# Two output projections of an encoder layer: norm weight applied while PSUM is emptied, scaling and residual in one operation, low parts of weights on another engine

## The chip, the cores and the metric

The kernel runs on one core of a Trainium2 chip. The metric is the device time of one execution in microseconds (us); times are medians over runs. The engines of a core, as the profile names them, are PE (TensorE, the matrix unit), DVE (VectorE), ACT (ScalarE), POOL (GpSimd) and SP (SyncE, which issues the DMAs here). Each engine works through its own queue in order; semaphores tie the queues together.

## The reference

One layer of an encoder trunk, 1024 tokens of width D = 1024, all in float32. Each of its three sub-layers stands between a norm before it and a norm behind it, and is added to the residual stream:

```
def _rms_norm(x, gain):
    y = x * rsqrt(mean(x * x, axis=-1) + EPS)
    return y * gain

mix = concat([attn_o, dn_o]) @ w_out            # mixer: windowed attention and DeltaNet
x = x + _rms_norm(mix, g_mix_post)
c = cross_attention(_rms_norm(x, g_cross_pre), _rms_norm(mem, g_mem), w_cq, w_ckv, w_co)
x = x + _rms_norm(c, g_cross_post)              # c ends with  o @ w_co
f = swiglu(_rms_norm(x, g_ffn_pre), w_gate_up, w_down)
x = x + _rms_norm(f, g_ffn_post)
```

The change concerns the two lines with `g_mix_post` and `g_cross_post`: the projections by `w_out` and `w_co` (1024 x 1024 each), the norm behind them and the residual addition.

## The kernel before

**Float32 in three products.** TensorE multiplies in a reduced format here. Each operand is split into a high part (a cast on ScalarE, line 102) and a low part (what is missing, line 103 or 106), and each product is made of three: high x high, high x low, low x high. A weight is loaded by `load_w` (lines 118 to 126): a DMA of 512 KB into `wraw`, a cast to `whi` on ScalarE, a subtraction to `wlo` on the engine that the caller names, VectorE if none. All three tiles have two buffers, and this happens with a priority 300 instructions ahead of the place where it stands in the program.

**The projection.** `mid_gemm` (lines 959 to 1000) does one half of the tokens (512, four tiles `z` of 128 tokens) for one projection. It is called four times: `w_out` halves 0 and 1, then, after the cross attention, `w_co` halves 0 and 1. Each call goes over two chunks `ch` of 512 output columns, and for each of them over four pieces `kp` of the weight; so there are 8 weight loads in a call and 32 in all, with `wlo` made by GpSimd. A chunk fills four PSUM banks (`pmg`). Each is then read twice: ScalarE squares it and sums the squares into one column of `sss[t]` (line 979), and VectorE copies it to `z` (line 980).

**The post norm.** After both chunks, for each of the four tiles: the residual `xr` is fetched (line 986); GpSimd adds the two sums (line 988) and forms `prs`, the reciprocal root of the mean, in two tiny operations (`rstd_of`, lines 157 and 158: scale and add EPS, then raise to -0.5); VectorE multiplies `z` by `prs` and by the gain `gpost` in one operation (line 991) and adds `xr` in another (line 992); `z` is written out (line 993). Then the next sub-layer's norm is prepared in the same loop: ScalarE squares `z` (line 995), GpSimd forms `pr` through the same two lines, and ScalarE scales into `xr` (line 998). `gpost` comes from `gpost_tile` (lines 952 to 955), a DMA that repeats the gain over 128 partitions. The same function serves the FFN's norm at the end of the kernel, where line 1300 multiplies the gain by sqrt(D); that norm leaves out the division by D in its statistics and has D x EPS instead (line 1328).

**What stands around it.** The normed tiles are transposed on TensorE (`ptn`) and split into operands. Between the halves lie the products of the cross attention: the query projection `cross_q` (`pcq`, line 254, with `wlo` from GpSimd), the scores `pcs`, their maximum and softmax (`cmx`, `cpr`, lines 1060 to 1068), the transposes `pct` with their split (`cph`, `cpl`) and `pco`. Behind the second call with `w_co`, the normed tiles become the FFN's operands T1 to T4 in a chain on VectorE and ScalarE (lines 1124 to 1141), while the first gate and up products are begun early (lines 1149 to 1171: `pA`, its copy `m`, the activation at line 1170). Then the FFN's main loop takes differences of weights (`pair_weights`, lines 1187 to 1211) and runs to the end.

**Order.** The order of instructions on each engine isn't written out by hand: a scheduler with its own estimates of durations lays it down when the kernel is built, so that a changed cost or engine can reorder what stands near it. `wraw`, `whi` and `wlo` have two buffers each, `z` and `xr` four, `pmg`, `pcq` and `pA` share four PSUM banks in this stage.

Of the kernel before, what the change touches and what calls it, by code (L numbers as in the profile page):

```python
# [10 lines left out]
F32 = mybir.dt.float32  # L11
# [3 lines left out]
ALU = mybir.AluOpType  # L15
# [4 lines left out]
P = 128  # L20
S = 1024
D = 1024
# [4 lines left out]
EPS = 1e-6  # L27
# [48 lines left out]
def tile_hybrid_block(  # L76
# [6 lines left out]
    nc = tc.nc  # L83
# [15 lines left out]
    def split(hi, lo, src, scale=None, eng=None):  # L99

        if scale is None:
            nc.scalar.copy(hi, src)  # L102
            (eng or nc.vector).tensor_tensor(lo, src, f32(hi), ALU.subtract)  # L103
        else:
            nc.scalar.activation(hi, src, AF.Identity, scale=scale)
            nc.vector.scalar_tensor_tensor(lo, src, scale, f32(hi), ALU.mult, ALU.subtract)

    def pool(name, bufs, **kw):
        return tc.tile_pool(name=name, bufs=bufs, reuse_waits="tile", **kw)
# [8 lines left out]
    def load_w(src, k, n, eng=None):  # L118

        with tc.high_priority(AHEAD):  # L120
            raw = wp.tile([P, k, n], F32, tag="wraw", name="wraw")
            nc.sync.dma_start(raw, src.rearrange("(k p) n -> p k n", p=P))
            hi = wp.tile([P, k, n], F32R, tag="whi", name="whi")
            lo = wp.tile([P, k, n], F32R, tag="wlo", name="wlo")
            split(hi, lo, raw, eng=eng)
        return hi, lo
# [4 lines left out]
    mhalf = cst.tile([P, 16], F32, name="mhalf")  # L131
# [22 lines left out]
    def rstd_of(rs, ss, n, eps):  # L154

        w = ss.shape[-1]
        nc.gpsimd.tensor_scalar(rs, ss, n, eps, ALU.mult, ALU.add)
        nc.gpsimd.tensor_tensor(rs, rs, mhalf[:, :w], ALU.pow)  # L158
# [31 lines left out]
    pss = ExitStack()  # L190
# [13 lines left out]
    for hf in range(2):  # L204
        hi = hx.tile([P, KT, HALF], F32R, name=f"hhi{hf}")
        lo = hx.tile([P, KT, HALF], F32R, name=f"hlo{hf}")
        for j in range(4):
            t = 4 * hf + j
# [4 lines left out]
            ss = t1.tile([P, 1], F32, tag="ss", name="ss", bufs=4)  # L213
            nc.scalar.activation(junk, xt, AF.Square, accum_out=ss)
            rs = t1.tile([P, 1], F32, tag="rs", name="rs", bufs=4)
# [88 lines left out]
    for hf in range(2):  # L304
        pp = pg.tile([P, 512], F32, tag="pg", name="pg")
# [644 lines left out]
            split(his[:, k, :], los[:, k, :], pt, gain(gname, k))  # L950

    def gpost_tile(pool_, g):
        t = pool_.tile([P, D], F32, tag="gpost", name="gpost", bufs=1)
        nc.sync.dma_start(t, g[0].partition_broadcast(P))
        return t

    XR = 4

    def mid_gemm(tz, act, w, gp, res, dst, hf, between=None):


        zs = [tz.tile([P, D], F32, tag="z", name="z", bufs=4) for _ in range(4)]
        sss = [tz.tile([P, 2], F32, tag="zss", name="zss", bufs=8) for _ in range(4)]
        for ch in range(2):
            cs = slice(ch * 512, (ch + 1) * 512)
            if ch and between:
                between()
            pp = [pg.tile([P, 512], F32, tag="pg", name="pmg") for _ in range(4)]
            for kp in range(4):
                whi, wlo = load_w(w[kp * 256:(kp + 1) * 256, cs], 2, 512, nc.gpsimd)  # L970
                for t in range(4):
                    tt = slice(t * P, (t + 1) * P)
                    for kk in range(2):
                        k = 2 * kp + kk
                        for i, (w_, a) in enumerate(((whi, 0), (whi, 1), (wlo, 0))):
                            nc.tensor.matmul(pp[t], act[a][:, k, tt], w_[:, kk, :], start=(k == 0 and i == 0),  # L976
                                             stop=(k == KT - 1 and i == 2))
            for t in range(4):
                nc.scalar.activation(zs[t][:, cs], pp[t], AF.Square, accum_out=sss[t][:, ch:ch + 1])
                nc.vector.tensor_copy(zs[t][:, cs], pp[t])  # L980
        xn = []
        for t in range(4):
            tok = slice(hf * HALF + t * P, hf * HALF + (t + 1) * P)
            z = zs[t]
            xr = tz.tile([P, D], F32, tag="xr", name="xr", bufs=XR)
            nc.sync.dma_start(xr, res[tok, :])
            ss = tz.tile([P, 1], F32, tag="pss", name="pss", bufs=4)
            nc.gpsimd.tensor_tensor(ss, sss[t][:, 0:1], sss[t][:, 1:2], ALU.add)
            rs = tz.tile([P, 1], F32, tag="prs", name="prs", bufs=4)
            rstd_of(rs, ss, 1.0 / D, EPS)  # L990
            nc.vector.scalar_tensor_tensor(z, z, rs, gp, ALU.mult, ALU.mult)
            nc.vector.tensor_tensor(z, z, xr, ALU.add)
            nc.sync.dma_start(dst[tok, :], z)
            s2 = tz.tile([P, 1], F32, tag="ps2", name="ps2", bufs=4)
            nc.scalar.activation(xr, z, AF.Square, accum_out=s2)
            r2 = tz.tile([P, 1], F32, tag="pr2", name="pr2", bufs=4)
            rstd_of(r2, s2, 1.0 / D, EPS)
            nc.scalar.activation(xr, z, AF.Identity, scale=r2)
            xn.append(xr)
        return xn  # L1000
# [6 lines left out]

    tz = L1.enter_context(pool("tz", 1))
    gp = gpost_tile(tz, g_mix_post)
    mxT = [s2_first[2:], [s2_first[1], opB3.tile([P, KT, HALF], F32R, tag="b3", name="b3")]]  # L1010

    raws = [opA.tile([P, KT, HALF], F32, tag=f"s0{i}", name="mraw") for i in range(2)]
    for hf in range(2):
        for kp in range(4):
# [3 lines left out]
                              .rearrange("(k p) t -> p k t", p=P))  # L1018
            split(mxT[hf][0][:, k2, :], mxT[hf][1][:, k2, :], raw[:, k2, :])
    xn0 = mid_gemm(tz, mxT[0], w_out, gp, x, d_x1, 0)  # L1020
    h2T = [operand(opA, "s0")]
    xn1 = mid_gemm(tz, mxT[1], w_out, gp, x, d_x1, 1, between=lambda: turn_norm(xn0, "cross", *h2T[0], pin=True))
    h2T.append(operand(opB, "s1"))
    turn_norm(xn1, "cross", *h2T[1])
# [75 lines left out]
    raw = tr.tile([P, KT, HALF], F32, name="xraw")  # L1100
    tz = L3.enter_context(pool("tz2", 1, side="right"))
    gp = gpost_tile(tz, g_cross_post)
    HK = KT // 2

    def blocks(t):
        return t[:, 0:HK], t[:, HK:KT]

    xn = mid_gemm(tz, q0, w_co, gp, d_x1, d_x2, 0)
    x1h, x1l = operand(opB, "s1")
    X11, X21 = (x1h[:, 0:HK], x1l[:, 0:HK]), (x1h[:, HK:KT], x1l[:, HK:KT])  # L1110
# [45 lines left out]
    for e in range(EARLY):  # L1156
        f = 2 * e
        sg = te.tile([P, 512], F32, tag="sg", name="sg0")
        w, A = [], []
        for i, c0 in enumerate((f * P, FF + f * P)):  # L1160
            whi, wlo = load_w(w_gate_up[:, c0:c0 + P], KT, P)
# [19 lines left out]
    def bank(name):  # L1181
        return pg.tile([P, 512], F32, tag="pg", name=name)
# [114 lines left out]
            late = last  # L1297
    with tc.issue_after(late.ins):
        gp = gpost_tile(keep, g_ffn_post)
    nc.scalar.mul(gp, gp, math.sqrt(D))  # L1300
    for t in range(NT):
        nc.vector.tensor_copy(z0[:, t], pps[t])
        jk = tp_.tile([P, 512], F32, tag="jk", name="jk", bufs=1)
# [2 lines left out]
    for t in range(NT):  # L1306
        tok = slice(t * P, (t + 1) * P)
        pp = bank("pd2")
# [12 lines left out]
        xr = tp_.tile([P, D], F32, tag="xrf", name="xrf", bufs=1)  # L1321
        with tc.issue_after(late.ins):
            nc.sync.dma_start(xr, d_x2[tok, :])
        z = tp_.tile([P, D], F32, tag="zf", name="zf")
        nc.scalar.activation(z[:, 512:], pp, AF.Square, accum_out=sq[:, 1, t:t + 1])

        rs = tp_.tile([P, 1], F32, tag="frs", name="frs")
# [38 lines left out]
```

## Time and profile before

| | us |
|---|---|
| median of three runs (lowest, highest) | 1670.23 (1670.08, 1673.58) |
| profiled execution, its own time | 1670.74 |
| its span, first to last instruction | 1669.0 |

Mean granted clock of TensorE in the profiled execution: 0.975 of full speed.

A timeline line of the profile has the start in us from the beginning of the span, the duration in us, the engine, the line of the kernel, the operation, the tile written and the tiles read (buffer numbers left out), and how many instructions were drawn together; in brackets stands how long the engine was idle before it, and whose signal ended that. A wait is put down to the signal that came last, which need not be its root.

### The profile page before, as it was taken

What the parts mean: (1) busy time and instruction counts of PE and PEld (TensorE: products, weight loads), DVE (VectorE), ACT (ScalarE), POOL (GpSimd) and SP (SyncE); (2) the same over time, 40 slices, a digit from 0 to 9 for tenths busy, and PEclk for the clock granted to TensorE, in tenths of its full rate; (3) what the DMA queues carried; (4) which work ended last, traced back from release to release, by engine and by line L of the source; (5) the groups of instructions that cost most, each with busy time, mean ns of one, the idle gap of its engine ahead of it and who ended that gap; (6) DMA issues with size and microseconds to landing.
All of it is one profiled execution on the core that took longest, in us unless ns stands there. A gap on an engine that the chain in (4) does not pass through costs nothing.

```text
span 1669.0 us, 21742 instructions
## 1 busy us (share of the span) xinstructions
PE 1569.7 (94%) x7802; PEld 1314.5 (79%) x7802; DVE 926.9 (56%) x1407; ACT 752.5 (45%) x1528; POOL 655.2 (39%) x557
## 2 busy tenths in 40 slices
PE   6989889997999879899999999999999999999998
PEld 5878778886888767678888777788888888888886
DVE  6754987876776543453335348677544554335342
ACT  6555553246867754554335555233323332445221
POOL 2467552344437534664225340334333332321010
PEclk9999999897999999999999999999999999999999
DMA  5134256665998456354222164343222223566452
GB/s 197 40 113 139 85 164 174 164 172 159 322 313 268 111 161 235 126 177 151 76 64 99 60 208 134 119 126 102 76 76 82 88 92 105 192 203 209 137 166 77
DMA packets 275560, 240.49 MB, mean 144 GB/s; under 512 B 43240, under 2 KB 226941, under 8 KB 275453
## 3 DMA queue, kind: packets, MB, share of 16 engines
q1 hardware_dynamic: 275453, 239.11, 46.0%
q8 instruction: 61, 1.00, 0.3%
q14 instruction: 46, 0.38, 0.1%
HBM read 177.69 MB, written 58.75 MB: 142 GB/s over the span
## 4 chain that ended last, share of the span: by engine, by line
PE 53%; POOL 3%; DMA 2%; DVE 2%; issue 2%; ACT 1%; SPq 0%; POOLq 0%; ACTq 0%
PE pd L1320 7%; PE pd L1295 7%; PE pD L1149 7%; PE pE L1149 7%; PE pA L1149 7%; PE pmg L976 6%; PE pcq L254 5%; PE pB L1149 3%; PE pco L1084 1%; PE pcs L1058 1%; POOL wlo L103 1%; DMA d_mv<-vv 1%; DMA mraw<-d_mix 1%; POOL prs L158 0%; POOL pr L158 0%
## 5 line engine op out<-in xcount | busy, mean ns | idle before, releaser
L103 POOL TENSOR_TENSOR wlo<-wraw,whi 128x1024 fp32r<-128x1024 f32 x88 | 217.5, 2473 | 294.8 <-ACT whi L102 281.5
L102 ACT CAST whi<-wraw 128x1024 fp32r<-128x1024 f32 x108 | 113.4, 1050 | 170.1 <-issue 74.9
L254 PE MATMUL pg<-hhi,whi 128*128 128x512 f32 x352 | 143.2, 408 | 0.0
L254 PE MATMUL pg<-hhi,wlo 128*128 128x512 f32 x352 | 142.1, 404 | 0.0
L254 PE MATMUL pg<-hlo,whi 128*128 128x512 f32 x352 | 142.1, 404 | 0.0
L976 PE MATMUL pmg<-whi,b 128*128 128x512 f32 x384 | 117.1, 400 | 7.4 <-ACT whi L102 5.2
L1149 PE MATMUL pA<-b,whi 128*128 128x512 f32 x352 | 111.2, 398 | 3.6 <-ACT m L1166 3.1
L279 DVE SCALAR_TENSOR_TENSOR acc<-cp,cols,acc 128x1024 f32<-128x1024 f32 x48 | 77.4, 1614 | 35.0 <-ACT acc L277 34.3
L1226 POOL TENSOR_TENSOR act<-act,up 128x512 f32<-128x512 f32 x33 | 47.8, 1449 | 114.5 <-issue 63.1
L976 PEld LDWEIGHTS pmg<-whi,b 128*128 128x128 f32 x384 | 73.3, 193 | 23.7 <-ACT whi L102 5.6
L1149 PEld LDWEIGHTS pA<-b,whi 128*128 128x128 f32 x352 | 66.4, 191 | 18.6 <-ACT m L1166 4.4
L254 PEld LDWEIGHTS pg<-hhi,wlo 128*128 128x128 f32 x352 | 68.4, 194 | 13.8
L254 PEld LDWEIGHTS pg<-hhi,whi 128*128 128x128 f32 x352 | 68.4, 195 | 13.5 <-ACT hhi L102 0.2
L254 PEld LDWEIGHTS pg<-hlo,whi 128*128 128x128 f32 x352 | 68.3, 194 | 13.4
L1198 POOL TENSOR_TENSOR sr<-wraw 128x512 f32<-128x512 f32 x22 | 28.5, 1297 | 115.9 <-DMA wraw<-in_w_gate_up_dram 107.3
L976 PE MATMUL pmg<-wlo,b 128*128 128x512 f32 x192 | 70.1, 395 | 1.3 <-POOL wlo L103 1.3
L1149 PE MATMUL pA<-b,wlo 128*128 128x512 f32 x176 | 69.6, 397 | 0.0
L1320 PE MATMUL pd<-wdh,ath 128*128 128x512 f32 x176 | 69.5, 395 | 0.0
L1320 PE MATMUL pd<-wdh,atl 128*128 128x512 f32 x176 | 69.5, 395 | 0.0
L1320 PE MATMUL pd<-wdl,ath 128*128 128x512 f32 x176 | 69.5, 395 | 0.0
L1295 PE MATMUL pd<-dl,whi 128*128 128x512 f32 x176 | 68.5, 389 | 0.0
L1295 PE MATMUL pd<-dh,wlo 128*128 128x512 f32 x176 | 68.4, 389 | 0.0
(392 smaller groups left out, 4222.1 us busy)
## 6 DMA issues: line engine op xcount, KB each, us to landing
wraw<-in_w_gate_up_dram SPq DMA_DIRECT2D x52, 512.0 KB, 4.0
kv<-d_kv SPq DMA_DIRECT2D x32, 512.0 KB, 6.2
wraw<-in_w_in_dram SPq DMA_DIRECT2D x22, 512.0 KB, 4.1
araw<-d_act SPq DMA_DIRECT2D x22, 512.0 KB, 3.4
draw<-in_w_down_dram SPq DMA_DIRECT2D x22, 512.0 KB, 4.4
atr<-d_act SPq DMA_DIRECT2D x16, 704.0 KB, 4.7
d_act<-act SPq DMA_DIRECT2D x40, 256.0 KB, 2.7
d_kv<-kv SPq DMA_DIRECT2D x8, 1024.0 KB, 6.3
```

The source lines that it names most:

```text
L102: nc.scalar.copy(hi, src)
L103: (eng or nc.vector).tensor_tensor(lo, src, f32(hi), ALU.subtract)
L254: nc.tensor.matmul(p_, w[:, k, :], ah[a][:, k, :], start=(k == 0 and i == 0), stop=(k == nk - 1 and i == 2))
L279: nc.vector.scalar_tensor_tensor(acc, cp[:, t:t + S], taps[t], acc, ALU.mult, ALU.add)
L976: nc.tensor.matmul(pp[t], act[a][:, k, tt], w_[:, kk, :], start=(k == 0 and i == 0), stop=(k == KT - 1 and i == 2))
L1058: nc.tensor.matmul(pp[:, t2_, :], q[a][:, ct, tt], kr_[b_][:, ct, :], start=(j == 0 and i == 0), stop=(j == 1 and i == 2))
L1084: nc.tensor.matmul(po, vr_[a][:, kt, cs], pts[kt][b_], start=(kt == 0 and i == 0), stop=(kt == 1 and i == 2))
L1149: nc.tensor.matmul(out_, w[a][:, k, :], xx[b_][:, k, :], start=(start and k == 0 and i == 0), stop=(k == HK - 1 and i == 2), skip_group_ch ...
L1198: nc.gpsimd.tensor_tensor(s[0], b_[:, 0:HK], b_[:, HK:], ALU.add)
L1226: nc.gpsimd.tensor_tensor(o_, o_, up, ALU.mult)
L1295: nc.tensor.matmul(pps[t], a[:, tt], b_, start=(f == 0 and i == 0), stop=(f == NF - 1 and i == 2))
L1320: nc.tensor.matmul(pp, a[:, f - f0], b_[:, f], start=(f == 0 and i == 0), stop=(f == NF - 1 and i == 2))
```

## The change

Five things are edited. (1) The low parts of the 32 weight tiles of `w_out` and `w_co` are made by VectorE instead of GpSimd. (2) When a PSUM bank is emptied into `z`, VectorE multiplies by the gain in place of copying; the squares are still taken of the unweighted bank. (3) The sum of the two partial sums of squares and the addition of EPS become one operation with two pointers, so that each tile has two tiny operations on GpSimd instead of three; the division by D is left out of the statistics, and (4) put as sqrt(D) into the gain, inside `gpost_tile`, which so has a multiplication on ScalarE for each of its three calls (the FFN's moves there from line 1300). (5) Scaling by `rs` and adding the residual are one operation on VectorE instead of two.

```
     def gpost_tile(pool_, g):
         t = pool_.tile([P, D], F32, tag="gpost", name="gpost", bufs=1)
         nc.sync.dma_start(t, g[0].partition_broadcast(P))
+        nc.scalar.mul(t, t, math.sqrt(D))
         return t
...
-                whi, wlo = load_w(w[kp * 256:(kp + 1) * 256, cs], 2, 512, nc.gpsimd)
+                whi, wlo = load_w(w[kp * 256:(kp + 1) * 256, cs], 2, 512)
...
             for t in range(4):
                 nc.scalar.activation(zs[t][:, cs], pp[t], AF.Square, accum_out=sss[t][:, ch:ch + 1])
-                nc.vector.tensor_copy(zs[t][:, cs], pp[t])
+                nc.vector.tensor_tensor(zs[t][:, cs], pp[t], gp[:, cs], ALU.mult)
...
             nc.sync.dma_start(xr, res[tok, :])
-            ss = tz.tile([P, 1], F32, tag="pss", name="pss", bufs=4)
-            nc.gpsimd.tensor_tensor(ss, sss[t][:, 0:1], sss[t][:, 1:2], ALU.add)
             rs = tz.tile([P, 1], F32, tag="prs", name="prs", bufs=4)
-            rstd_of(rs, ss, 1.0 / D, EPS)
-            nc.vector.scalar_tensor_tensor(z, z, rs, gp, ALU.mult, ALU.mult)
-            nc.vector.tensor_tensor(z, z, xr, ALU.add)
+            nc.gpsimd.tensor_scalar(rs, sss[t][:, 1:2], sss[t][:, 0:1], D * EPS, ALU.add, ALU.add)
+            nc.gpsimd.tensor_tensor(rs, rs, mhalf[:, 0:1], ALU.pow)
+            nc.vector.scalar_tensor_tensor(z, z, rs, xr, ALU.mult, ALU.add)
             nc.sync.dma_start(dst[tok, :], z)
...
         gp = gpost_tile(keep, g_ffn_post)
-    nc.scalar.mul(gp, gp, math.sqrt(D))
```

## The prediction

> **What bounds the kernel now.** First the page's busy line: TensorE works for 94% of the span, no other engine for more than 56%. The time can only fall where TensorE stands still, or runs at half clock, around the edited lines.
>
> ```profile
> PE 1569.7 (94%) x7802; PEld 1314.5 (79%) x7802; DVE 926.9 (56%) x1407; ACT 752.5 (45%) x1528; POOL 655.2 (39%) x557
> ```
>
> Second, what TensorE waited for between 640 and 1060 us, where both output projections, the cross attention and the early gate/up products lie (total, times, longest). All lines together come to 25.8 us; after 1060 us no wait of TensorE is over 0.2 us.
>
> ```profile
> PE pmg L976 <- ACT whi L102: 5.2, 1, 5.2
> PE pB L1149 <- DVE x L106: 3.8, 1, 3.8
> PE pB L1149 <- ACT s1h L102: 3.3, 1, 3.3
> PE pA L1149 <- ACT m L1166: 3.1, 3, 2.7
> PE pcq L254 <- POOL wlo L103: 1.6, 2, 1.2
> PE pmg L976 <- POOL wlo L103: 1.3, 2, 1.1
> ```
>
> Third, the windows around those waits (busy time of TensorE, its weight loads, VectorE, ScalarE and GpSimd, then the granted clock). The clock falls below 1.00 exactly behind long waits.
>
> ```profile
> 686.00:698.00 12.00, 6.79 (x24) 5.18 (x23) 1.87 (x2) 7.31 (x10) 7.25 (x7) 0.86 0.47 179
> 922.00:932.00 10.00, 6.72 (x23) 4.46 (x23) 3.50 (x8) 5.53 (x13) 2.38 (x1) 0.83 0.24 75
> 985.00:997.00 12.00, 8.06 (x24) 5.89 (x24) 5.11 (x6) 10.04 (x14) 2.19 (x6) 0.72 0.59 199
> ```
>
> A clock of 0.86 over 12 us is 1.7 us lost; 0.83 over 10 is 1.7; 0.72 over 12 is 3.4. Two more windows (1029 to 1041 and 1045 to 1055) have 0.86 and 0.83, 1.7 each. Together 10.2 us, so the ceiling for anything this change can win is 25.8 + 10.2 = 36 us.
>
> Fourth, the timeline of the first post norm, to see why the longest wait is there.
>
> ```profile
> 676.24 1.28 DVE L991 SCALAR_TENSOR_TENSOR z<-z,prs,gpost 128x1024 f32<-128x1024 f32 x1
> 676.39 1.18 POOL L157 TENSOR_SCALAR prs<-pss 128x1 f32<-128x1 f32 x1
> 677.65 1.40 POOL L158 TENSOR_TENSOR prs<-prs,mhalf 128x1 f32<-128x1 f32 x1
> ...
> 679.02 2.37 POOL L103 TENSOR_TENSOR wlo<-wraw,whi 128x1024 fp32r<-128x1024 f32 x1
> 679.17 3.30 DVE L991 SCALAR_TENSOR_TENSOR z<-z,prs,gpost 128x1024 f32<-128x1024 f32 x1
> ...
> 687.17 1.15 ACT L998 ACTIVATE xr<-z,pr 128x1024 f32<-128x1024 f32 x1 [7.33 <-POOL pr L158]
> ...
> 691.35 1.03 ACT L102 CAST whi<-wraw 128x1024 fp32r<-128x1024 f32 x1
> ```
>
> The wait's row names the high part `whi`, but the cause sits upstream. GpSimd's subtract `wlo` (2.37 us) and VectorE's product (1.28 us alone) collide and the product takes 3.30; GpSimd's next tiny additions queue behind; ScalarE idles 7.33 us for `pr` with the next `whi` queued behind that scaling. So GpSimd, only 39% busy, sets TensorE's longest wait.
>
> **The change, part by part.** The groups that price it (line, engine, operation, count | busy us, mean ns | idle before):
>
> ```profile
> L103 POOL TENSOR_TENSOR wlo<-wraw,whi 128x1024 fp32r<-128x1024 f32 x88 | 217.5, 2473 | 294.8 <-ACT whi L102 281.5 <-DMA pz<-d_pz 6.8 <-PE pcs L1058 3.3
> L103 DVE TENSOR_TENSOR wlo<-wraw,whi 128x1024 fp32r<-128x1024 f32 x20 | 25.5, 1276 | 25.9 <-ACT whi L102 25.8
> L991 DVE SCALAR_TENSOR_TENSOR z<-z,prs,gpost 128x1024 f32<-128x1024 f32 x16 | 24.5, 1538 | 1.1 <-POOL prs L158 1.1
> L992 DVE TENSOR_TENSOR z<-z,xr 128x1024 f32<-128x1024 f32 x16 | 22.4, 1418 | 0.0
> L1249 DVE TENSOR_TENSOR v<-a,pB 128x512 f32<-128x512 f32 x22 | 15.0, 683 | 12.0 <-PE pB L1149 8.6 <-ACT a L1246 3.4
> ```
>
> *Low parts.* 32 of GpSimd's 88 subtracts go to VectorE: 32 x 2.4 = 77 us leave GpSimd, 32 x 1.22 (the undisturbed case) = 39 us come to VectorE.
>
> *Norm.* The 16 additions of L992 vanish (16 x 1.22 = 19.5 us of VectorE); the product of L991 stays one operation over two SBUF tiles (now `z` and `xr`), 1.28 us. VectorE's net is +19.5 us, on an engine with 44% idle.
>
> *Emptying PSUM.* The copy of L980 (687 ns) becomes a product of PSUM and SBUF; the nearest row, L1249, has that form at 683. Zero; 32 x 4 ns is 0.1 us either way.
>
> *Statistics.* One of GpSimd's three tiny operations per tile goes (0.19 us alone; 1.17 at 681.35 when VectorE is busy): 16 x 0.2 = 3 us off a chain of which only the norms' part counts, and is counted below. The two-pointer form is not in this stage; the FFN's own norm has it at 0.30 alone and 1.14 beside VectorE, so a loss of up to 0.1 per tile or a gain of 1.
>
> *Gains times sqrt(D).* Two new ScalarE multiplications, 1.06 us each by the FFN's row at L1300. The first stands behind `vv` at 621.1, where ScalarE idles until 624.2; the gain's DMA is issued at 617.1 and takes some 5.4 us, so it is hidden, or costs at most 1.06. The second, near 773, waits for its DMA until about 776 and holds the next `whi` (775.9 before), the copies from `pcq` and the softmax's exponentials behind it for some 1.2 us; TensorE has products queued until about 781, which hide it. Without that cover: 1.2.
>
> *Residual.* The product now waits for `xr`, one operation earlier than the addition did. In the second half of the first projection `xr` lands at 729.8, 731.1, 733.4 and 736.4; I put the products at 729.7, 731.5, 734.9 and 736.8. Zero, at most 0.1.
>
> Now the places, in order. I followed each by hand with the order of instructions that the change builds and the undisturbed durations.
>
> A, 651.7: VectorE's split of `vr` takes 3.56 us beside GpSimd's subtract and delays the emptying of PSUM. The wait is 1.18; gain **1.2** (0 to 1.2).
>
> B, 672 to 698: with GpSimd free, the four products run at 674.5, 675.8, 679.5 and 680.8, the squares end by 683.1, the scalings by 686.6, and the next `whi` by 687.6 instead of 692.4: 4.8 us, plus 1.5 of half clock. Gain **6.3** (4 to 7.5).
>
> C, 736 to 745: waits of 0.4 and 1.2 on the query projection's `wlo`, which stays on GpSimd, pushed there by stretched statistics. Gain **0.8** (-1 to 1.6).
>
> D, 905 to 932: VectorE is busy for 15.2 of 17 us up to 922, GpSimd's `wlo` takes 4.33 at 915.2, an addition 2.84. The softmax's exponentials at 921.5 move to about 918. Waits of 0.8, 1.4, 1.3 and 0.5, and half clock of 1.7: ceiling 5.7, gain **4** (2 to 5.5).
>
> E, 976 to 1055: `xr` of the last tile is ready about 991.5 instead of 998.4, as four additions (4.9 us) and the stretched powers (1.40 to 1.54 where 0.54 is the row alone) leave the chain; the operands T1 to T4, 31 to 35 us of VectorE's work, start 7 us earlier. Waits of 3.95, 3.8 and 3.25 and half clock of 6.8 are the ceiling, 17.8. I leave 2.8 + 1.2 + 1.7 of the waits, since early `wlo` still share VectorE with the norm, and a third of the half clock: gain **10** (4 to 13).
>
> The trace has half clock of 3.4 us also behind 2.7 us of waiting at 987.5 and behind the split waits near 924, so waits left over may still cost half clock. The Trainium skill, "TensorE: Matmul & The Clock Gate" (Part 1: The HAM clock gate), has the clock halved after an idle window of about 3.4 us that runs freely; by it the leftovers would cost no half clock unless they met such a window, some 2 us more gain at E; the trace is harsher, and the sum goes by the trace.
>
> Sum: 1.2 + 6.3 + 0.8 + 4 + 10 = 22.3. The profiled execution took 1670.74 us (span 1669.0), 0.5 above the median of 1670.23. 1670.7 - 22.3 = 1648.4; I take **1650**, rounding up for waits that hand work misses.
>
> **The rivals.** *Half the gain.* VectorE's operations with two SBUF tiles hold up GpSimd's tiny statistics (0.54 to 1.40 and 1.53 near 675 to 678), and after the change VectorE has more of them: 48 instead of 32. If each of the eight pairs in a norm is 1 us late, and ScalarE's queue, in which all eight squares and scalings now stand ahead of the next two `whi`, waits with them, B's `whi` ends at about 690 (gain 2 to 3) and E gives 4 to 5; A, C and D give 4: some 10, **1661**. Against it: GpSimd's own 2.4 us subtracts, which did most of the damage, are gone from these stretches. The Trainium skill, "SBUF — State Buffer" (Who interferes with whom), speaks against the change here: a VectorE instruction with two SBUF inputs and a GpSimd one that reads SBUF exclude each other for the whole of whichever starts first. The stretched rows agree (3.30 for 1.28, and 1.40 for 0.54); by it this rival's 1661 is the time.
>
> *Slower: low parts block VectorE.* Each moved `wlo` waits for its `whi`, and that waits until TensorE lets go of one of two buffers. On VectorE, a queue in order, the emptying of PSUM, `cpl` and the softmax's maximum stand behind it; GpSimd had nothing urgent there. If 16 of 32 lie so that TensorE's next input is 1.22 us late each, that is 19.5, against the 10 of the rival above: **1680**. It decides when `whi` ends later than the input of VectorE's next operation. Against it: between 838 and 900 eight `whi` (840.4 to 898.0) plus 1.05 and 1.22 end before VectorE's next operation by 0 to 1.2 us, so the slack is thin.
>
> *No change.* The queue of weight DMAs and the split of weights for the early products (L1194 to L1201) bind 1032 and 1046 instead, and ScalarE's order binds B: **1670**.
>
> **How the numbers follow.** The runs shown differ by 0.2% among themselves, 3.4 us, which is about what a measurement can tell here. My sum 0.56, half the gain 0.25, slower 0.14, no change 0.05. So faster 0.81, same 0.05, slower 0.14. The range goes from 1640 (the sum of the upper bounds is 28.8, 1642, and 2 for error) to 1667, which leaves out no change, the slower case and little else; on its own the likeliest case spans 1640 to 1657.
>
> **What would show it.** Right: no wait of `pmg` for `whi` above 1 us near 687, the granted clock 1.00 in 686 to 698 and 922 to 932, the last `xr` near 991, no wait near 1046, and no stretched rows of L991 by GpSimd. Half right: powers at 1.4 throughout both norms, and `whi` at 690. Wrong: new waits of TensorE whose releaser is VectorE's `wlo`, `z` or `cpl`, spread over 650 to 985, about 1 us each.

## The result, and the profile after

The changed kernel takes 1647.47 us (median of 4 runs, 1644.75 to 1650.78) against 1670.15 for the kernel before beside it: a ratio of 0.986, 95% interval 0.9845 to 0.9874, or 22.7 us less. The forecast was 1650, in the range 1640 to 1667, faster. So the size of the gain was right. Its cause was only partly what the prediction named; the experiments show that.

The profiled execution after took 1644.75 us, 26.0 less than the one before. Not all of that is the change's: TensorE's first product of the projections (`pmg`) starts at 626.13 us where it started at 627.78, and up to there the same work is done in both. Half-clock stretches ahead of the projections add up to anything from 41 to 72 us in the profiles of this study, and the first `pmg` product starts anywhere from 623.84 to 637.66 us, mostly the later the more half clock there was. That moves the whole time by several us from run to run. **The stretch** from the start of the first `pmg` product to the start of the last product of the kernel leaves most of that out: 1032.8 us before and 1008.4 after, 24.4 less. A second profile of each gave 1032.1 and 1008.7. The experiments are compared by this stretch, which repeated within 1 us in these two pairs, and by the medians, which don't repeat so well. It isn't wholly free of the clock: some profiles begin it with about 3 us at half clock (both of the changed kernel, one of the two of before), others at full clock. TensorE then comes up to 1.6 us earlier to a wait for `z` near 650, ahead of any norm, and waits longer there; in three runs of those below (low parts alone, gain apart, all scalings on VectorE) half clock followed that wait, and the stretch is 1.2 to 2.3 us longer by then than in the other profiles.

The page's busy line after:

```profile
PE 1558.2 (95%) x7802; PEld 1306.5 (80%) x7802; DVE 938.0 (57%) x1423; ACT 753.3 (46%) x1530; POOL 567.3 (35%) x509
```

VectorE has 11 us more to do, not the 19.5 of the sum: some 5 of the other 8 us is stretching of the norms' operations that is gone. GpSimd has 88 us less. The waits of TensorE after, 630 to 1060 us (total, times, longest):

```profile
PE pmg L978 <- ACT whi L102: 2.2, 1, 2.2
PE pA L1149 <- ACT m L1166: 1.3, 2, 0.7
PE pA L1149 <- DVE wlo L103: 1.1, 2, 0.5
PE pB L1149 <- DVE s1l L103: 1.0, 1, 1.0
...
PE pmg L978 <- DVE z L982: 0.7, 1, 0.7
...
PE pB L1149 <- ACT s1h L102: 0.5, 1, 0.5
```

The 5.2 has become 2.2, the 3.8 and 3.3 of `pB` are 1.0 and 0.5, and no wait for a `wlo` from GpSimd is left. What VectorE's new work holds up is small (`wlo` 1.1 in two waits). The windows that answer to the three shown of before have the full clock throughout (PEclk, the number behind the five busy times and their counts):

```profile
682.00:694.00 12.00, 9.77 (x43) 7.76 (x42) 3.59 (x3) 6.12 (x8) 1.23 (x3) 1.00 0.26 90
906.00:916.00 10.00, 8.85 (x43) 6.71 (x42) 5.54 (x11) 4.22 (x12) 0.00 (x0) 1.00 0.32 104
966.00:978.00 12.00, 10.85 (x50) 8.35 (x49) 3.59 (x5) 10.92 (x14) 3.44 (x7) 1.00 0.61 214
```

The account closes to about 1 us. Idle time of TensorE inside the stretch (gaps over 0.15 us) fell from 25.8 to 10.3 us, half clock from 23.4 to 3.4 us, half of which is lost time: 15.5 + 10.0 = 25.5, against 24.4.

The first norm after, in the timeline:

```profile
676.21 2.47 DVE L992 SCALAR_TENSOR_TENSOR z<-z,prs,xr 128x1024 f32<-128x1024 f32 x2
676.47 1.42 POOL L158 TENSOR_TENSOR pr<-pr,mhalf 128x1 f32<-128x1 f32 x1
...
682.53 2.19 ACT L998 ACTIVATE xr<-z,pr 128x1024 f32<-128x1024 f32 x2
...
684.62 1.98 ACT L102 CAST whi<-wraw 128x1024 fp32r<-128x1024 f32 x2
```

VectorE's last operation of this norm ends at 678.7, where it was 687.9 before. By equal counts of TensorE's products the kernel is 2.3 us ahead when it comes to this norm, so VectorE is 6.9 us faster in it. The next `whi` ends at 685.7 instead of 692.4, 4.4 us faster by the same account, because ScalarE still has squares and scalings ahead of it: that is the 2.2 us wait that is left. The groups that priced the change:

```profile
L103 POOL TENSOR_TENSOR wlo<-wraw,whi 128x1024 fp32r<-128x1024 f32 x56 | 137.5, 2456 | 202.5 <-ACT whi L102 202.3
L103 DVE TENSOR_TENSOR wlo<-wraw,whi 128x1024 fp32r<-128x1024 f32 x52 | 64.8, 1248 | 90.9 <-ACT whi L102 86.8 <-PE ptn L947 2.5 <-PE pct L1074 1.5
L992 DVE SCALAR_TENSOR_TENSOR z<-z,prs,xr 128x1024 f32<-128x1024 f32 x16 | 22.2, 1412 | 2.4 <-POOL prs L991 2.1 <-DMA xr<-in_x_dram 0.2
L982 DVE TENSOR_TENSOR z<-pmg,gpost 128x512 f32<-128x512 f32 x32 | 21.5, 685 | 7.6 <-ACT z L981 7.6
```

### The profile page after: what moved, and what is told of

The parts are those of the page before. It is cut to its first block, busy times and chain, and to the rows that moved or that the text cites. A ratio compares the mean times of both kernels' runs of the same rounds, so it can differ in the third digit from the quotient of the medians.

```text
span 1643.0 us, 21684 instructions
## 1 busy us (share of the span) xinstructions
PE 1558.2 (95%) x7802; PEld 1306.5 (80%) x7802; DVE 938.0 (57%) x1423; ACT 753.3 (46%) x1530; POOL 567.3 (35%) x509
## 4 chain that ended last, share of the span: by engine, by line
PE 55%; DMA 2%; DVE 2%; ACT 1%; issue 1%; SPq 0%; POOL 0%; POOLq 0%; ACTq 0%; DVEq 0%
PE pmg L978 9%; PE pd L1319 7%; PE pd L1295 7%; PE pE L1149 7%; PE pD L1149 7%; PE pA L1149 6%; PE pcq L254 5%; PE pB L1149 3%; PE pcs L1058 1%; PE pco L1084 1%; DMA wraw<-in_w_gate_up_dram 1%; DMA mraw<-d_mix 1%; DMA d_mv<-vv 0%; PE ptn L947 0%; PE pct L1074 0%
## 5 line engine op out<-in xcount | busy, mean ns | idle before, releaser
L103 POOL TENSOR_TENSOR wlo<-wraw,whi 128x1024 fp32r<-128x1024 f32 x56 | 137.5, 2456 | 202.5 <-ACT whi L102 202.3
L103 DVE TENSOR_TENSOR wlo<-wraw,whi 128x1024 fp32r<-128x1024 f32 x52 | 64.8, 1248 | 90.9 <-ACT whi L102 86.8
```

## The experiments

**The theory on trial.** The prediction read GpSimd as the root: its subtracts of 2.4 us hold up VectorE's products and its own statistics. The rival: VectorE's own queue is what the norms wait for, so that the merged operations bring the gain. The edit was taken apart.

*The low parts alone.*

```
-                whi, wlo = load_w(w[kp * 256:(kp + 1) * 256, cs], 2, 512, nc.gpsimd)
+                whi, wlo = load_w(w[kp * 256:(kp + 1) * 256, cs], 2, 512)
```

> The kernel before with one edit: the 32 low parts of the projections' weights by VectorE; copy, statistics, product and addition as before. Theory (GpSimd's subtract of 2.4 us is the root: it holds up VectorE's products and GpSimd's own statistics): 10 to 16 us less than before, about 1657, although VectorE has 39 us more to do. The waits of TensorE for a low part from GpSimd are gone, and no L991 near 3.3 us is left in the first norm. Rival (the merged operations on VectorE bring the gain, and moving the low parts onto VectorE by itself only loads it): less than 4 us gained, or slower.

Measured: 1663.24 us, ratio 0.9943 (0.9915 to 0.9971); stretch 1026.5, so 6.3 of the 24.4. GpSimd's subtracts of these weights are gone, and L991 averages 1279 ns instead of 1538, as foreseen; yet less is won than the theory asked. The window of the first norm shows VectorE as full as before, in the first fence of the kernel before, in the second of this one (after the length stand the busy times of TensorE, its weight loads, VectorE, ScalarE and GpSimd):

```profile
673.80:687.90 14.10, 12.31 (x53) 9.50 (x51) 13.32 (x11) 4.22 (x9) 12.65 (x13) 1.00 0.47 157
```

```profile
678.80:692.80 14.00, 13.45 (x59) 10.81 (x58) 13.23 (x13) 7.38 (x14) 10.75 (x15) 1.00 0.52 181
```

VectorE is busy for 13.2 of 14.0 us with GpSimd's subtract gone, as it was for 13.3 of 14.1 with it. (The first window leaves out the norm's first copy, at 672.94; from the first copy to the last addition it is 14.9 us before and 13.9 here.) A good part of the time that GpSimd no longer takes from it, its own low part takes. TensorE's waits (total, times, longest) that are left: the softmax's `cpr` on VectorE is late, `whi` in the first norm still comes 2.4 us late, and one low part of the query projection, still GpSimd's, too:

```profile
PE pct L1074 <- DVE cpr L1068: 3.1, 2, 2.8
...
PE pcq L254 <- POOL wlo L103: 2.4, 1, 2.4
PE pmg L976 <- ACT whi L102: 2.4, 1, 2.4
```

*All but the low parts.* The changed kernel with `nc.gpsimd` put back in the line above.

> The changed kernel with the low parts back on GpSimd. Theory: 6 to 11 us less than before, about 1661; the first norm (672 to 735) still has a wait of TensorE for whi of 2 us or more, and the products of 1.28 us are still stretched to 3.3. Rival (the merged operations bring it): 18 us or more less than before, within 5 us of the changed kernel. If the two parts add up, the gains of this run and of the one with the low parts alone sum to about 23.

Measured: 1655.72 us, ratio 0.9905 (0.9879 to 0.9931), stretch 1016.6: 16.2 of the 24.4. That lies between the two forecasts, by the stretch nearer to the rival's. TensorE's wait for `whi` in the first norm is 1.4 us, under the 2 that the theory asked, though one merged operation there still takes 2.82 us beside GpSimd's subtract. The parts nearly add up: 6.3 + 16.2 = 22.5 of 24.4, so the low parts are worth 6.3 by themselves and 8.2 once the operations are merged.

*Only the product and the merged operation,* with low parts and statistics as before:

```
-                nc.vector.tensor_copy(zs[t][:, cs], pp[t])
+                nc.vector.tensor_tensor(zs[t][:, cs], pp[t], gp[:, cs], ALU.mult)
...
-            nc.vector.scalar_tensor_tensor(z, z, rs, gp, ALU.mult, ALU.mult)
-            nc.vector.tensor_tensor(z, z, xr, ALU.add)
+            nc.vector.scalar_tensor_tensor(z, z, rs, xr, ALU.mult, ALU.add)
```

> The kernel before with the gain multiplied in as PSUM is emptied and scaling and residual in one operation; low parts on GpSimd, statistics in three tiny operations and without sqrt(D) as before. It differs from the run with only the low parts put back by the statistics and the two multiplications of the gain. My sum gave these nearly nothing (16 x 0.2 us, off the path but for the norms): within 2 us of that run. A rival in which the tiny operations stretched to 1.2 us each hold the norms: 3 to 6 us slower than that run.

Measured: 1656.63 us, ratio 0.991 (0.9875 to 0.9946), stretch 1017.9: 14.9 us won. The statistics and the two multiplications of the gain are worth 1.3 us together, within the 2 expected. GpSimd's subtract still does its harm here, and 14.9 us are won all the same: the merged operation averages 1600 ns where it would be 1280, and stands idle for 7.5 us for `prs`.

```profile
L991 DVE SCALAR_TENSOR_TENSOR z<-z,prs,xr 128x1024 f32<-128x1024 f32 x16 | 25.6, 1600 | 7.9 <-POOL prs L158 7.5 <-DMA xr<-in_x_dram 0.3
```

*The changed kernel again,* beside these three.

> The changed kernel once more, beside the others on one chip: 20 to 25 us less than before. If its spread comes from half clock before the projections, the stretch from the first product of the projection to the end is the same to 1 us as in its first profile.

Measured: 1648.13 us (1642.77 to 1649.39), ratio 0.9852 (0.9824 to 0.988), stretch 1008.7.

**The new theory: VectorE's own operations in the norms.** As stated ahead of the runs: VectorE's queue is what the norms wait for. Two runs take it apart from its rivals. *The gain multiplied in apart,* so that VectorE's work is long again, but not the chain behind `prs`:

```
-                nc.vector.tensor_tensor(zs[t][:, cs], pp[t], gp[:, cs], ALU.mult)
+                nc.vector.tensor_copy(zs[t][:, cs], pp[t])
...
             nc.sync.dma_start(xr, res[tok, :])
+            nc.vector.tensor_tensor(z, z, gp, ALU.mult)
             rs = tz.tile([P, 1], F32, tag="prs", name="prs", bufs=4)
```

> The changed kernel, but PSUM is emptied by a copy and the gain is multiplied in by an operation of its own (128x1024, 1.22 us) ahead of the statistics' use: low parts on VectorE, statistics and the fused scaling and residual as changed. VectorE has the same number of operations as with the low parts alone, but the chain behind the reciprocal root stays one operation long. Measured as the stretch from the first product of the projections (pmg) to the last product of the kernel: 1032.8 before, 1026.5 with the low parts alone, 1008.4 changed. New theory (VectorE's queue is what the norms wait for, so any operation of 1.2 us per tile there costs alike): 1022 to 1027. Rival (only the chain behind the root counts, since VectorE can do the gain while it waits): 1008 to 1012. My prediction's reading (GpSimd's subtract is the root, and it is on VectorE here): 1008 to 1014.

Measured: 1661.31 us, ratio 0.9933 (0.9919 to 0.9948), stretch 1023.6. Sixteen operations, 19.2 us of VectorE's time, cost 15.3 us of the stretch, though none of them waits for `prs`. Some 2.1 us of the 15.3 lie at the wait near 650, ahead of the norms, so 13.2 are the edit's. That is the new theory's forecast; the one about the chain and the prediction's own reading (1008 to 1014) are out.

```profile
L989 DVE TENSOR_TENSOR z<-z,gpost 128x1024 f32<-128x1024 f32 x16 | 19.2, 1221 | 0.1
```

How such an operation costs so much, the run doesn't settle. It can make VectorE's later work late, as its queue is in order; or it can hold up GpSimd's tiny statistics, which stretch beside it, and with them ScalarE. The rows of ScalarE's scaling, after and here (where the line has moved by one), speak for the second:

```profile
L998 ACT ACTIVATE xr<-z,pr 128x1024 f32<-128x1024 f32 x16 | 18.2, 1149 | 4.6 <-POOL pr L158 4.6
L999 ACT ACTIVATE xr<-z,pr 128x1024 f32<-128x1024 f32 x16 | 18.1, 1150 | 18.4 <-POOL pr L158 18.4
```

ScalarE's waits for `pr` grew from 4.6 to 18.4 us, and the same 64 tiny operations of GpSimd took 48.0 us instead of 38.4. In the first norm, counted from VectorE's first operation on a PSUM bank, ScalarE's first square starts 0.4 us later than in the changed kernel, and the scaling that waits for `pr` 2.0 us later. So there the larger part came by way of GpSimd.

*The addition left out of the kernel before* (line 992 removed; no other edit).

> The kernel before without the residual addition of L992 (left out, so the projections' residual is missing from the stream): low parts on GpSimd, statistics, product and copy as before. If VectorE's 16 operations of 1.22 us are what the fused form saves, the stretch is that of the run with product and residual fused, 1017.9, within 2 us. If instead something else in that edit (the gain's place, the earlier wait for the residual) brings it, the stretch stays above 1024.

Measured in one profile: stretch 1018.4, against 1017.9 with both operations fused. So the fused form saves what the addition cost, and the gain's new place and the earlier wait for `xr` cost nothing that these profiles can tell, as the prediction had them.

**Does any VectorE work cost that much?** *The query projection's low parts moved too:*

```
-            whi, wlo = load_w(w_cq[:, ct * P:(ct + 1) * P], KT, P, nc.gpsimd)
+            whi, wlo = load_w(w_cq[:, ct * P:(ct + 1) * P], KT, P)
```

> The changed kernel with the 16 low parts of the query projection's weights on VectorE as well. GpSimd's last subtracts among the norms go (one holds two products of the second norm for 4.62 instead of 2.5 us), VectorE has 16 x 1.22 = 19.5 us more. New theory: TensorE has no wait left for pcq in the changed kernel, so nothing can be won there, and where VectorE's queue binds each 1.22 may cost: stretch 1008 to 1013. Old reading (GpSimd's subtract is the root): 1005 to 1008.

Measured: 1650.16 us, ratio 0.9865 (0.9848 to 0.9881), stretch 1009.4. Some 19.5 us more of VectorE's work, as much as cost 13 to 15 us inside the norms, costs 1.0 here, hardly more than the stretch varies by itself. Place decides, not amount. The 1.0 is net of whatever the move of GpSimd's last subtracts out of the norms won, which can't be told apart here.

*The scaling by `pr` on VectorE,* behind the products instead of among them:

```
-            nc.scalar.activation(xr, z, AF.Identity, scale=r2)
+            nc.vector.tensor_scalar(xr, z, r2, None, ALU.mult)
```

> The changed kernel with the scaling by pr (L998, 16 x 1.15 us on ScalarE) on VectorE. In the changed kernel TensorE's longest wait, 2.2 us at 683.5, ends with a whi that stands behind two such scalings on ScalarE while VectorE is idle for 7 us. There this wins up to 2 us. Everywhere else VectorE gets 16 more operations, 0.6 to 1.2 us each. If VectorE's queue is the bound of the norms: net 0 to 8 us slower, stretch 1008 to 1016. If ScalarE's order is by now the bound: 1003 to 1007.

Measured: 1644.32 us, ratio 0.9837 (0.9814 to 0.986), stretch 1008.6, the changed kernel's. The wait for `whi` near 683 is gone, and three others came: 2.9 us for `z` at 653 with half clock behind it, and 0.7 and 1.0 for the scaled `xr` in the second norm. The one at 653 is not the edit's, since no scaling stands ahead of it: `z` came 25.0 us after the first product (24.4 and 24.7 in the two profiles of the changed kernel), but TensorE came there 1.6 us earlier, its stretch having begun at full clock. By equal counts of products the run is 2.2 us behind the changed kernel up to 660, wins 2.2 from there to 735 and 1.9 after 960, and loses 2.2 between 735 and 800. *The same for the last two tiles of each norm only* (`if t >= 2`):

> The changed kernel with the scaling by pr on VectorE for the last two of the four tiles of each norm, ScalarE for the first two. The time of VectorE counts in the norms where its queue is full, up to the last product; behind that it idles, and the scaling takes 0.76 us there against 1.15 on ScalarE. So theory: the wait for whi at 683.5 (2.2 us) is gone or under 0.5, and no new wait at the other norms: stretch 1004 to 1008 (1008.4 changed). If the kernel has no slack on VectorE at the ends of the norms either: 1009 to 1014.

Measured: 1648.53 us, ratio 0.9859 (0.9828 to 0.989), stretch 1007.5, with no wait near 683. *And in the first norm only* (`if dst is d_x1 and hf == 0`):

> The changed kernel with the scaling by pr on VectorE in the first norm alone (first projection, first half). What the run with all scalings moved gave back (a wait of 2.9 us at 653 and half clock behind it) stands ahead of any norm. If it comes from the order that the scheduler lays down or from when the transfers land, it may come here too; if it comes from the scalings themselves, it can't, as none stands ahead of 653. Theory (ScalarE's order is what the last wait in the first norm is made of): the wait near 683 gone, stretch 1005 to 1008.

Measured: 1645.93 us, ratio 0.9845 (0.9825 to 0.9865), stretch 1006.5: 1.9 us less than changed, the wait near 683 gone and 0.9 at 652. In the stretch this is the expected 2 us; in the medians nothing can be told from the changed kernel.

*All scalings on VectorE, and the low parts of the memory's keys and values on GpSimd,* to be rid of the wait at 653:

```
-        split(*hl, raw)
+        split(*hl, raw, eng=nc.gpsimd)
```

> The kernel with all scalings by pr on VectorE (stretch 1008.6), and the low parts of the memory's keys and values (two subtracts of 2.3 us on VectorE between 640 and 656) on GpSimd, which since the change has nothing to do there. The wait of TensorE at 653 for VectorE to empty PSUM (2.9 us, and 1.7 of half clock) should go: stretch 1003 to 1006, time 3 to 6 us under the changed kernel. If the wait at 653 is ScalarE's (its casts of the same tiles) and not VectorE's, the stretch stays at 1008 to 1009.

Measured: 1645.94 us, ratio 0.985 (0.9816 to 0.9884), stretch 1006.3, short of the 3 to 6 us. The wait is still 2.2 us, and still for VectorE's `z`, now without half clock behind it. `z` came 24.3 us after the first product instead of 25.0; that and the half clock make up the 2.3 us between this stretch and that of the run with all scalings moved. So VectorE's work ahead of `z` did count, but the move brought back the collision:

```profile
655.60 4.63 POOL L103 TENSOR_TENSOR kr<-mkr,kr 128x2048 fp32r<-128x2048 f32 x1 [32.34 <-ACT kr L102]
656.50 4.80 DVE L103 TENSOR_TENSOR wlo<-wraw,whi 128x1024 fp32r<-128x1024 f32 x1 [1.53 <-ACT whi L102]
```

VectorE's `wlo`, 1.22 us alone, was taken up at 656.50, when GpSimd's subtract had begun, and ended at 661.30, 1.07 us after that subtract's end at 660.23.

*The kernel before once more,* for its profile.

> The kernel before, for one more profile. All shares of the edits were read as differences of the stretch from the first product of the projections to the last product, from one profile of before (1032.8 us). If the stretch is a property of the kernel, it is 1032 to 1034 again, while the time as a whole may differ by several us; if it varies like the time as a whole, shares of 1 to 2 us can't be told.

Measured: 1666.22 us in one run, stretch 1032.1.

## Why the prediction was right, and where its reasons were not

**The places.** By equal counts of TensorE's products (7802 in every kernel), what each stage of the stretch won, beside the forecast:

| stage of before, us | forecast | measured | low parts alone | product and merged operation alone |
|---|---|---|---|---|
| A, to 660 | 1.2 | 0.7 | -1.2 | 0.3 |
| B, to 735 | 6.3 | 5.8 | 3.3 | 6.1 |
| C, to 800 | 0.8 | 2.2 | -1.9 | 1.1 |
| D, 905 to 960 | 4 | 4.7 | 0.3 | 3.5 |
| E, 960 to the end | 10 | 11.1 | 5.8 | 3.9 |

Sum 22.3 against 24.4. Between 800 and 905 nothing changes. The clock after was better than taken: no half clock at all behind the first 3.4 us of the stretch, where the sum had left some at B and E. C was mis-sized: the two waits went entirely, and as spacings between TensorE's products they were 1.9 us, not 1.6; the last 0.3 us comes from counting products that stand in another order there. At B the forecast of no wait over 1 us failed by the 2.2 that is left. `whi` came nearly when it was forecast (688.0 by the clock of before, against 687.6); TensorE came there 1.4 us earlier, because its wait of 1.1 us for `wlo` at 680 was gone. The gain is the forecast's two terms, 4.4 and 1.4 us for 4.8 and 1.5.

**The parts.** The PSUM product took 685 ns against 687 for the copy, as priced. The statistics and the two multiplications by sqrt(D) came out at 1.3 us won; the first multiplication ran from 621.23 to 622.29 in ScalarE's idle time, the second at 764.92 with the next `whi` behind it at 765.88, and no wait of TensorE answers to either. The last `xr` of the last norm was ready at 976.8; set back by the 15.0 us that the kernel is ahead when it comes to that norm, that is 991.8 on the clock of before, against the forecast 991.5 and 998.4 before.

**The step that failed** is the fourth view, "So GpSimd, only 39% busy, sets TensorE's longest wait." The chain was read from the row before the wait to GpSimd's subtract, whose collision is the most visible thing in it. But VectorE had 13.3 of 14.1 us filled in the same window, and a product stretched by 2.0 us is a small part of that. Taking GpSimd's subtracts out left VectorE as full and won 6.3; taking the additions out won 14.4 to 14.9. At B, where that wait stands, the merged operation won all of the stage's gain with GpSimd's subtract still in place, and the low parts alone little over half of it (the table's last columns). The reading isn't wrong everywhere: at E the low parts alone won 5.8 of 11.1, more than the merged operation. The sum came out right all the same, since the hand schedule was drawn with all parts of the change at once, and in it VectorE had become free; that a right sum went with this reading of the wait is, to that extent, luck.

**The rivals.** *Half the gain* assumed powers at 1.4 us throughout. Some did stay stretched after the change (1.38, 1.37, 1.42 us in the first norm, the other five 0.55 to 0.57; the group of `prs` went from 827 to 881 ns, that of `pr` from 760 to 658), and in the second norm the query projection's subtract on GpSimd still takes two products of VectorE from 2.5 to 4.62 us. But VectorE waits for `prs` only 2.1 us in all 16 tiles, and `whi` in B came at 685.7, or 688.0 by the clock of before, against 687.6 forecast and 690 in this rival. The Trainium skill, "SBUF — State Buffer" (Who interferes with whom), has the two engines exclude each other for a whole instruction; the rows agree, and the `wlo` of 4.80 us above most clearly. That it would halve the gain was wrong, because little of what is stretched so is still waited for: ScalarE's waits for `pr` fell from 23.2 us before to 4.6.

*Slower, low parts block VectorE:* the waits for `wlo` from VectorE are 1.1 us in all, and the run with 16 more of them lost 1.0. In the kernel with the low parts alone, part of this rival is real: the wait for `cpr` (3.1) is VectorE's lateness. It didn't decide, since the merged operations paid for the room. *No change* is refuted by the result: the waits at 1032 and 1046 became 1.0 and 0.5 us, though nothing about the weight transfers was edited.

Still open: how much of the 14.9 us is each operation's own 1.22 us and how much the different order that the scheduler lays down with fewer operations; no run held the order fixed. Open too is how much of an operation's cost in the norms goes through VectorE's queue and how much through GpSimd's statistics: the additions, the product put in apart and the low parts all read two SBUF tiles, and no run put in operations of the same length beside which GpSimd's don't stretch.

## What to carry to other kernels

Where a wait is traced upstream, sum the busy time of every engine in the window of the wait: an engine that is 56% busy over the span can be 94% busy in the 14 us that count, and then an operation on it there can cost most of its length, whatever it waits for itself (19.2 us of work cost 13 to 15), while as much work elsewhere cost next to nothing (19.5 us cost 1.0). A visible collision is not yet the root: take it out alone, and see whether the engine behind it gets idle. And to compare small edits, cut the unchanged part of the run away, compare the stretch in which they lie, and then stage by stage: a wait ahead of the edit moved a whole stretch by 2 us.

## What the hardware showed unexpectedly

Short waits of TensorE were followed by 3.4 us at half clock in some kernels and not in others: waits of 2.4 and 2.6 us with the low parts alone were, and even pieces of 1.1 and 0.5 us with the addition left out; one of 2.2 us in the changed kernel was not, nor one of 2.5 us (at 1014) in the kernel with the merged operation alone. And VectorE scales a 128x1024 tile by one pointer in 0.76 us, where ScalarE takes 1.15 and VectorE's own operations on two tiles 1.22 to 1.28.
